# Decoder layer: twenty sets of weight sums instead of ten, formed in DRAM by accumulating DMAs

## Chip, cores and metric

The kernel runs on one core of one Trainium2 chip. The metric is the device time of one execution in microseconds; lower is better.

## The reference

One decoder layer in float32 on 256 tokens of width 2048: a SwiGLU feed-forward (inner width 5632), a mixer (sliding-window attention beside an RWKV-7 recurrence), cross-attention into a memory of 256 tokens, and a second feed-forward.

```python
def swiglu(h, w_gate, w_up, w_down):
    return (jax.nn.silu(h @ w_gate) * (h @ w_up)) @ w_down
...
x = x + 0.5 * swiglu(rms_norm(x, ffn1_norm[l]), ffn1_w_gate[l], ffn1_w_up[l], ffn1_w_down[l])
x = gated_parallel_mixer(x, ...)
x = memory_cross_attention(x, mem, ...)
x = x + 0.5 * swiglu(rms_norm(x, ffn2_norm[l]), ffn2_w_gate[l], ffn2_w_up[l], ffn2_w_down[l])
return rms_norm(x, final_norm)
```

## The kernel before

**Three-pass products.** Every product of activations and weights is made of three matmuls. Both factors are split into a high part (`hi`, rounded to the matmul's float32r format by ScalarE, L400) and a rest (`lo`, L401, VectorE), and `times` (L477 to L479) multiplies hi by hi, lo by hi and hi by lo into one accumulator bank. A matmul is 128 x 128 by 128 x 512.

**Items.** The weights come from DRAM in units of two row chunks (128 rows each) by 512 columns, split as they come. In the feed-forwards the gate and the up matrix (or two column blocks of the down matrix) are worked together. There an *item* is a pair of such units, `g` and `u`, and multiplies two row chunks with two token halves: four block products of two chunks, 8 x 3 = 24 matmuls. A block of 512 columns has eight items, q = 0 to 7. `next_item` prepares one item ahead of TensorE.

**Seven products.** For some q (`SEVEN` in the first feed-forward, `SEVEN_2` in the second) the 2 x 2 block product is made with seven products instead of eight, in the manner of Strassen and Winograd: 21 matmuls. That needs four sums of the weight chunks (`divide`, L429 to L432, VectorE), which are split in turn (`two_parts`, L408 and L409, tiles `thi` and `tlo`, one buffer each), and sums of the activations, made once (`combinations`, L509 to L528, tile parts `chi` and `clo`). The products go to the banks p1 to p7; `middle` (L614 to L616) and `out` (L623 to L628) put them together. `x` holds the first feed-forward's or the second's token block, and `rs` is the reciprocal root of the norm, made on GpSimd (L714) and read by Silu (L753 in the first column block, L624 in the others).

**Staged sums.** In the second feed-forward, q = 3 of each of ten column blocks (`STAGED`) doesn't form its sums in place. They were formed during the mixer: `stage` loads the gate's and the up matrix's chunks into two tiles (L380), makes four subtractions on VectorE (L384 to L389) and stores the four sums to the DRAM tensor `sums` (L392). `load_sums` (L369) loads them two items ahead into two `raw` buffers of a ring of four, which the sums formed in place and the activations' sums use too.

**Order.** All weights are loaded by SP's queue, in one order, into four `raw2` buffers of 1 MB in the feed-forwards. Side work is written as generators that `Interleave` steps between the items of the main work (`bg.spawn`, `bg.tick`); `stage` is one of them and begins at item `STAGE_AT`. The stepping sets where an instruction is recorded. The framework then places the instructions on each engine's queue by its own order, with waits for data and buffers; it holds an instruction back only where `issue_after` names one to wait behind. GpSimd's queue has, in the first feed-forward, the constants, `rs`, the fetches of the small vectors (L254, L293) and the stores of x (L828).

Of the kernel before, what the change touches and what calls it, by code (L numbers as in the profile page):

```python
# [8 lines left out]
F32R = mybir.dt.float32r  # L9
# [127 lines left out]
def decoder_layer(ctx: ExitStack, tc: tile.TileContext, a: dict, out: bass.AP):  # L137
# [175 lines left out]
    for entry in weight_plan(a):  # L313
        if entry is None:
            ends.append(len(units))
            continue
        plan.append(entry)
        w, k0, nk, c0, n = entry
        if not isinstance(w, tuple):
            for k in range(k0, k0 + nk, KU):  # L320
                items.append(((len(units),), False))
                units.append((w, k, c0, n))
            continue
        for k in range(k0, k0 + nk, 2 * KU):
            u = len(units)
            units += [(v, k + i, c, 512) for v, c in zip(w, c0) for i in (0, KU)]
            for i in range(2):
                q = (k - k0) // KU + i
                if n == SEVEN_2 and q in STAGED:
# [3 lines left out]
    first_unused = {items[i][0][1] for i in staged}  # L333
    sums_d = dram.tile([len(staged), P, 4, 512], F32, name="sums")
    at = {"item": 0, "product": 0, "pool": None}

    def load(u, pieces=None):

        if u >= len(units) or u in raws:
            return  # L340
        w, k, c0, n = units[u]
        wide = at["pool"] is not None and (u < ends[0] or u >= ends[1] + LOADED)
        m = 2 if wide else 1
        if wide:
            raw = at["pool"].tile([P, m * KU, n], F32, tag="raw2", name="raw2", bufs=4)
# [4 lines left out]
        if u in first_unused:  # L350
            second = u + 1 in first_unused
            pieces = [(slice(1, 2), nc.sync)] + [(slice(2 + second, 4), nc.sync)]
            if not second:
                pieces = ((slice(1, 4), nc.sync),)
        elif u + 1 in first_unused and wide:
            pieces = ((slice(0, 2), nc.sync), (slice(3, 4), nc.sync))
        for i, queue in pieces or ((slice(0, m * KU), nc.sync),):
            rows = slice((k + i.start) * P, (k + i.stop) * P)
            queue.dma_start(raw[:, i], w[rows, c0 : c0 + n].rearrange("(a p) n -> p a n", p=P))

    def load_sums(i):

        if i not in staged or i in summed:
            return
        summed[i] = [
            wp.tile([P, KU, 512], F32, tag="raw", name="raw", bufs=4) for _ in range(2)
        ]
        for e, t in enumerate(summed[i]):
            nc.sync.dma_start(t[:], sums_d[staged[i], :, KU * e : KU * e + KU, :])  # L369

    def stage(t4, i, n):


        while at["item"] < STAGE_AT[n]:
            yield
        t = t4("su", (P, KU, 512)), t4("sg", (P, KU, 512))
        for e, v in zip(t, items[i][0][::-1]):
            w, k, c0, _ = units[v]
            rows = slice(k * P, (k + KU) * P)
            nc.sync.dma_start(e[:], w[rows, c0 : c0 + 512].rearrange("(a p) n -> p a n", p=P))  # L380
        yield from idle(4)
        u0, u1, g0, g1 = (e[:, c] for e in t for c in range(KU))
# [3 lines left out]
        yield  # L386
        with tc.issue_after(at["lo"].ins):
            dve.tensor_tensor(u1, u1, g0, ALU.subtract)
            dve.tensor_tensor(g1, g1, u1, ALU.subtract)  # L389
        yield from idle(8)  # L390
        for c, e in enumerate(t):
            nc.sync.dma_start(sums_d[n, :, KU * c : KU * c + KU, :], e[:])  # L392

    def split_unit(u, rows=slice(0, KU)):
        n, raw = units[u][3], raws[u]
# [5 lines left out]
            at["lo"] = dve.tensor_tensor(lo[:, s], raw[:, s], f32(hi[:, s]), ALU.subtract)  # L401
        return hi, lo

    def two_parts(v, e):
        sp = at["pool"]
        hi = sp.tile([P, KU, 512], F32R, tag="thi" + e, name="thi")
        lo = sp.tile([P, KU, 512], F32R, tag="tlo" + e, name="tlo")
        act.copy(hi[:], v[:])  # L408
        dve.tensor_tensor(lo[:], v[:], f32(hi[:]), ALU.subtract)  # L409
        return hi, lo  # L410

    def divide(i):


        if i >= len(items) or i in parts:
            return
        which, seven = items[i]
        if len(which) == 1:
            parts[i] = split_unit(*which)
            return  # L420
        g, u = which
        if not seven:
            parts[i] = split_unit(g), split_unit(u)
            return
        t = summed.get(i)
        if t is None:
            rg, ru = raws[g], raws[u]
            t = [wp.tile([P, KU, 512], F32, tag="raw", name="raw", bufs=4) for _ in range(2)]
            dve.tensor_tensor(t[1][:, 0], ru[:, 0], rg[:, 0], ALU.subtract)  # L429
            dve.tensor_tensor(t[0][:, 0], ru[:, 1], ru[:, 0], ALU.subtract)  # L430
# [58 lines left out]
    def combinations(sp, x: Act, seven, name, ready=lambda: True, early=True, n=0):  # L489
# [8 lines left out]
        def work():  # L498
# [3 lines left out]
            for q in pairs:  # L502
# [9 lines left out]
                    )  # L512
                if q in seven:
                    n = 4
                    dve.tensor_tensor(f[:, 0], v[:, 0, 1], v[:, 1, 1], ALU.add)
                    dve.tensor_tensor(f[:, 1], f[:, 0], v[:, 0, 0], ALU.subtract)
                    dve.tensor_tensor(f[:, 2], v[:, 0, 0], v[:, 0, 1], ALU.subtract)
# [19 lines left out]
    def product_pair(x: Act, c, w, first, middle, out):  # L537
# [28 lines left out]
        for q in range(nk // KU):  # L566
            k = KU * q
            if q in seven:
# [2 lines left out]
                end = q == max(seven)  # L571
                ta, tb = s
                for i, (to, x_, w_) in enumerate((
                    ("p7", of_c(q, 2), of_w(ta, 0)), ("p6", of_c(q, 1), of_w(ta, 1)),
                    ("p1", of_x(0, k), of_w(g, 0)), ("p2", of_x(0, k + 1), of_w(g, 1)),
                    ("p3", of_c(q, 3), of_w(u, 1)), ("p4", of_x(1, k + 1), of_w(tb, 1)),
                    ("p5", of_c(q, 0), of_w(tb, 0)),
                )):
                    add(to, x_, w_, end and to in ("p1", "p5", "p6", "p7"))
                    if i % 2:  # L580
                        bg.tick()
                    if end and to == "p1":
                        first(b)
# [21 lines left out]
    def gate_and_up(sp, x: Act, c, r, w):  # L605
# [5 lines left out]
            act.copy(hb[:, 0], b["p1"][:])  # L611

        def middle(b):
            dve.tensor_tensor(u2[:], b["p6"][:], hb[:, 0], ALU.add)  # L614
# [5 lines left out]
        def out(b, to):  # L620
            t = int(to in ("p4", "p5"))
            if to in ("p2", "p4"):
                dve.tensor_tensor(hb[:, t], b[to][:], u3[:] if t else hb[:, 0], ALU.add)  # L623
# [9 lines left out]
    def down(sp, h: Act, c, w, xs):  # L633

        u2, u3 = sums_of(sp)

        def half(x_, v):
            dve.scalar_tensor_tensor(x_, v, 0.5, x_, ALU.mult, ALU.add)

        def first(b):  # L640
            act.copy(u3[:], b["p1"][:])
# [1 line left out]
            half(xs[1][1], b["q"][:])  # L643

        def middle(b):
            dve.tensor_tensor(u2[:], b["p6"][:], u3[:], ALU.add)
            dve.tensor_tensor(u3[:], b["p7"][:], u2[:], ALU.add)
            dve.tensor_tensor(u2[:], b["p5"][:], u2[:], ALU.add)
            half(xs[1][0], u3[:])
            half(xs[1][1], u3[:])  # L650
            half(xs[0][1], u2[:])

# [65 lines left out]
    def feed_forward(sp, x, norm: Norm, wg, wu, wd, done, begin_last=lambda: None, last=False):  # L718
        if last:
            for tag, shape, dt, bufs in (  # L720
                ("hhi", [P, 16, T], F32R, 1), ("hlo", [P, 16, T], F32R, 1),
                ("hb", [P, 2, 512], F32, 2), ("thia", [P, KU, 512], F32R, 1),
                ("tloa", [P, KU, 512], F32R, 1), ("thib", [P, KU, 512], F32R, 1),
                ("tlob", [P, KU, 512], F32R, 1),
            ):
                sp.tile(shape, dt, tag=tag, name=tag, bufs=bufs)
        begun = at["item"]
# [76 lines left out]
    with tc.tile_pool(name="f1", bufs=1, reuse_waits="tile") as sp:  # L804
# [32 lines left out]
    with tc.tile_pool(name="mx", bufs=1, reuse_waits="tile") as sp:  # L837
# [6 lines left out]
        for i, n in staged.items():  # L844
            bg.spawn("stage", stage(t4, i, n))

        def act_tiles(name, n):
            return Act(
# [845 lines left out]
```

## Time and profile before

| | |
|---|---|
| time, median of 3 runs | 2246.25 us (2245.61 to 2247.01) |
| span of the profiled execution, first to last instruction | 2242.8 us |
| median less that span | 3.45 us |
| TensorE busy | 2228.0 us, 10587 matmuls |
| VectorE busy | 1824.9 us |
| ScalarE busy | 1248.6 us |
| GpSimd busy | 129.8 us |
| moved by DMA | 461.84 MB, mean 206 GB/s |
| granted TensorE clock | 0.999 |

The page gives the profiled execution's time as its span alone; what lies around it is in the difference to the median. A busy share of TensorE counts overlapping matmuls, so the rate is read from their starts in the timeline. A row of the windows gives, for each engine, the busy time in that stretch with the number of instructions, then the granted clock, the busy share of the DMA engines and GB/s.

### The profile page before, as it was taken

What the parts mean: (1) busy time and instruction counts of PE and PEld (TensorE: products, weight loads), DVE (VectorE), ACT (ScalarE), POOL (GpSimd) and SP (SyncE); (2) the same over time, 40 slices, a digit from 0 to 9 for tenths busy, and PEclk for the clock granted to TensorE, in tenths of its full rate; (3) what the DMA queues carried; (4) which work ended last, traced back from release to release, by engine and by line L of the source; (5) the groups of instructions that cost most, each with busy time, mean ns of one, the idle gap of its engine ahead of it and who ended that gap; (6) DMA issues with size and microseconds to landing.
All of it is one profiled execution on the core that took longest, in us unless ns stands there. A gap on an engine that the chain in (4) does not pass through costs nothing.

```text
span 2242.8 us, 28283 instructions
## 1 busy us (share of the span) xinstructions
PE 2228.0 (99%) x10587; PEld 1830.8 (82%) x10587; DVE 1824.9 (81%) x2365; ACT 1248.6 (56%) x1629; POOL 129.8 (6%) x197
## 2 busy tenths in 40 slices
PE   9999999999999999999999999999999999999998
PEld 7888888888888877788888888888888888888886
DVE  7898988998989476977657656547999999999997
ACT  6555555555556468544434546456565466555654
POOL 1000000000001001200321030001000000000000
PEclk9999999999999999999999999999999999999999
DMA  7555555555555544676668576547565566556564
GB/s 264 188 199 197 204 195 201 203 189 206 193 201 197 170 137 152 193 233 212 207 214 281 194 260 231 188 167 272 199 234 205 199 231 220 201 200 227 197 226 150
DMA packets 229705, 461.84 MB, mean 206 GB/s; under 512 B 15467, under 2 KB 17744, under 8 KB 229568
## 3 DMA queue, kind: packets, MB, share of 16 engines
q1 hardware_dynamic: 220512, 433.62, 56.7%
q0 software_dynamic: 8592, 25.62, 3.7%
q8 instruction: 83, 1.36, 0.2%
q10 hardware_dynamic: 464, 0.79, 0.1%
q14 instruction: 54, 0.44, 0.1%
HBM read 436.30 MB, written 23.59 MB: 205 GB/s over the span
## 4 chain that ended last, share of the span: by engine, by line
PE 97%; DVE 1%; DMA 1%; issue 1%; ACT 0%; SPq 0%; POOL 0%; POOLq 0%; DVEq 0%
PE acc L477 20%; PE acc L478 19%; PE acc L479 19%; PE mm L478 8%; PE mm L479 8%; PE mm L477 8%; PE tr L665 2%; PE tr L478 2%; PE tr L477 2%; PE tr L479 2%; PE mm L1349 1%; PE tr L1285 1%; DVE lo L401 0%; PE mm L912 0%; DMA raw<-in_ffn_w_gate_dram 0%
## 5 line engine op out<-in xcount | busy, mean ns | idle before, releaser
L400 ACT CAST hi<-raw 128x1024 fp32r<-128x1024 f32 (+1 forms) x770 | 756.2, 992 | 710.3 <-PE acc L479 509.5
L401 DVE TENSOR_TENSOR lo<-raw,hi 128x1024 fp32r<-128x1024 f32 (+1 forms) x770 | 882.4, 1149 | 307.7 <-ACT hi L400 306.0
L477 PE MATMUL acc<-hi,xhi 128*128 128x512 f32 (+1 forms) x1166 | 461.4, 396 | 2.5 <-ACT xhi L692 2.1
L478 PE MATMUL acc<-lo,xhi 128*128 128x512 f32 (+1 forms) x1166 | 452.9, 388 | 0.0
L479 PE MATMUL acc<-hi,xlo 128*128 128x512 f32 (+1 forms) x1166 | 452.4, 388 | 0.0
L477 PEld LDWEIGHTS acc<-hi,xhi 128*128 128x128 f32 x1166 | 219.3, 188 | 50.6 <-issue 4.0
L479 PEld LDWEIGHTS acc<-hi,xlo 128*128 128x128 f32 x1166 | 218.8, 188 | 45.7 <-DVE xlo L693 1.0
L478 PEld LDWEIGHTS acc<-lo,xhi 128*128 128x128 f32 x1166 | 219.2, 188 | 43.8 <-issue 1.7
L408 ACT CAST thi<-raw 128x1024 fp32r<-128x1024 f32 x192 | 199.7, 1051 | 62.2 <-DVE raw L431 41.8
L409 DVE TENSOR_TENSOR tlo<-raw,thi 128x1024 fp32r<-128x1024 f32 x192 | 232.3, 1219 | 1.2 <-ACT thi L408 0.4
L479 PE MATMUL acc<-hi,hlo 128*128 128x512 f32 x372 | 145.5, 391 | 0.0
L478 PE MATMUL acc<-lo,hhi 128*128 128x512 f32 x372 | 145.4, 391 | 0.0
L477 PE MATMUL mm<-hi,xhi 128*128 128x512 f32 x370 | 145.4, 393 | 0.0
L477 PE MATMUL acc<-hi,hhi 128*128 128x512 f32 x372 | 144.9, 390 | 0.0
L479 PE MATMUL mm<-hi,xlo 128*128 128x512 f32 x370 | 144.3, 390 | 0.0
L478 PE MATMUL mm<-lo,xhi 128*128 128x512 f32 x370 | 144.2, 390 | 0.0
L478 PEld LDWEIGHTS acc<-lo,hhi 128*128 128x128 f32 x372 | 69.9, 188 | 14.3
L477 PEld LDWEIGHTS acc<-hi,hhi 128*128 128x128 f32 x372 | 69.9, 188 | 14.3
L479 PEld LDWEIGHTS acc<-hi,hlo 128*128 128x128 f32 x372 | 69.9, 188 | 14.0
L479 PEld LDWEIGHTS mm<-hi,xlo 128*128 128x128 f32 x370 | 69.4, 188 | 14.5
L478 PEld LDWEIGHTS mm<-lo,xhi 128*128 128x128 f32 x370 | 69.5, 188 | 14.2
L477 PEld LDWEIGHTS mm<-hi,xhi 128*128 128x128 f32 x370 | 69.5, 188 | 14.1
(410 smaller groups left out, 3601.1 us busy)
## 6 DMA issues: line engine op xcount, KB each, us to landing
raw<-in_ffn_w_down_dram SPq DMA_DIRECT2D x88, 1024.0 KB, 5.2
raw<-in_ffn_w_gate_dram SPq DMA_DIRECT2D x84, 1024.0 KB, 5.1
raw<-in_ffn_w_up_dram SPq DMA_DIRECT2D x78, 1024.0 KB, 6.4
raw<-in_w_in_dram SPq DMA_DIRECT2D x136, 512.0 KB, 3.5
raw<-in_w_out_dram SPq DMA_DIRECT2D x32, 512.0 KB, 4.4
raw<-sums SPq DMA_DIRECT2D x20, 512.0 KB, 6.2
raw<-in_w_proj_attn_dram SPq DMA_DIRECT2D x16, 512.0 KB, 3.9
raw<-in_w_proj_rwkv_dram SPq DMA_DIRECT2D x16, 512.0 KB, 5.6
```

Of the source, the lines that this page charges most:

```text
L400: at["hi"] = act.copy(hi[:, s], raw[:, s])
L401: at["lo"] = dve.tensor_tensor(lo[:, s], raw[:, s], f32(hi[:, s]), ALU.subtract)
L408: act.copy(hi[:], v[:])
L409: dve.tensor_tensor(lo[:], v[:], f32(hi[:]), ALU.subtract)
L477: pe.matmul(o, xh, hi, start=first, stop=False, **how)
L478: pe.matmul(o, xh, lo, start=False, stop=False, **how)
L479: pe.matmul(o, xl, hi, start=False, stop=last, **how)
L665: pe.transpose(b[:, o : o + P], tok[:, t, col : col + P], ident[:])
L1285: pe.matmul(b[e][:, o : o + P], x1[r, j, cs_], x2[r, j, cs_], start=True, stop=True)
L1349: pe.matmul(vb[:, (o + k) * P : (o + k + 1) * P][:, r], lhs(k, e), rhs[:, k, r], start=first and k + e == 0, stop=True, **ek,)
```

## The change

The second feed-forward has seven products in five of eight items (q = 0, 2, 3, 4, 5) instead of four, in each of ten column blocks. The sums of two of them, q = 3 and q = 5, are staged: twenty sets.

The sums are not formed during the mixer any more, on VectorE, but from the first feed-forward on, by DMAs from DRAM to DRAM on GpSimd's queue, some of them accumulating into their target. A set takes eight DMAs of 256 KB in six steps: t1 <- u0 and t3 <- u0; t1 += g0 and t3 += u1; t2 <- t1; t2 += u1; t4 <- t2; t4 += g1. The generators begin at items 18, 23, and so on to 113 of the first feed-forward.

An accumulating DMA only adds, so the signs of the weights' sums change everywhere, and those of the activations' sums and of the put-together with them. t1 takes the place of the chunk u0 that the seven products don't use (in place, L429, or loaded there from `sums`), so `u` is now split whole and the second tile of sums has one chunk instead of two.

```diff
-SEVEN_2, STAGED = (0, 2, 3, 4), (3,)
+SEVEN_2, STAGED = (0, 2, 3, 4, 5), (3, 5)
-STAGE_AT = [266 + 2 * n for n in range(10)]
+STAGE_AT = [18 + 5 * n for n in range(20)]
...
+        for v in first:
+            nc.sync.dma_start(raws[v][:, 0], sums_d[first_sums[v], :, 0, :])
...
-        for e, t in enumerate(summed[i]):
-            nc.sync.dma_start(t[:], sums_d[staged[i], :, KU * e : KU * e + KU, :])
+        for t, c, m in zip(summed[i], (1, 3), (2, 1)):
+            nc.sync.dma_start(t[:, :m], sums_d[staged[i], :, c : c + m, :])
-    def stage(t4, i, n):
+    def stage(i, n):
         while at["item"] < STAGE_AT[n]:
             yield
-        t = t4("su", (P, KU, 512)), t4("sg", (P, KU, 512))
-        for e, v in zip(t, items[i][0][::-1]):
-            ...
-            nc.sync.dma_start(e[:], w[rows, c0 : c0 + 512].rearrange("(a p) n -> p a n", p=P))
...
-        with tc.issue_after(at["lo"].ins):
-            dve.tensor_tensor(g0, u0, g0, ALU.subtract)
-            dve.tensor_tensor(u0, u1, u0, ALU.subtract)
...
-        for c, e in enumerate(t):
-            nc.sync.dma_start(sums_d[n, :, KU * c : KU * c + KU, :], e[:])
+        t1, t2, t3, t4 = (sums_d[n, :, c, :] for c in range(4))
...
+        for steps in (
+            ((t1, u0), (t3, u0)), ((t1, g0), (t3, u1)), ((t2, t1),), ((t2, u1),), ((t4, t2),),
+            ((t4, g1),),
+        ):
+            for to, of in steps:
+                if of is u0 or of is t1 or of is t2:
+                    pool.dma_start(to, of)
+                else:
+                    pool.dma_start(to, of, accum_op=ALU.add)
+            yield from idle(8)
...
-            dve.tensor_tensor(t[1][:, 0], ru[:, 0], rg[:, 0], ALU.subtract)
-            dve.tensor_tensor(t[0][:, 0], ru[:, 1], ru[:, 0], ALU.subtract)
-            dve.tensor_tensor(t[0][:, 1], ru[:, 1], t[1][:, 0], ALU.subtract)
-            dve.tensor_tensor(t[1][:, 1], rg[:, 1], t[0][:, 1], ALU.subtract)
-        a_ = two_parts(t[0], "a")
-        parts[i] = split_unit(g), split_unit(u, slice(1, 2)), (a_, two_parts(t[1], "b"))
+            dve.tensor_tensor(ru[:, 0], ru[:, 0], rg[:, 0], ALU.add)
+            dve.tensor_tensor(t[0][:, 0], ru[:, 1], ru[:, 0], ALU.add)
+            dve.tensor_tensor(t[0][:, 1], t[0][:, 0], rg[:, 0], ALU.subtract)
+            dve.tensor_tensor(t[1][:, 0], t[0][:, 0], rg[:, 1], ALU.add)
+        a_ = two_parts(t[0], "a", 2)
+        parts[i] = split_unit(g), split_unit(u), (a_, two_parts(t[1], "b", 1))
...
                 for i, (to, x_, w_) in enumerate((
-                    ("p7", of_c(q, 2), of_w(ta, 0)), ("p6", of_c(q, 1), of_w(ta, 1)),
+                    ("p7", of_c(q, 2), of_w(ta, 1)), ("p6", of_c(q, 1), of_w(ta, 0)),
...
-                    ("p3", of_c(q, 3), of_w(u, 1)), ("p4", of_x(1, k + 1), of_w(tb, 1)),
-                    ("p5", of_c(q, 0), of_w(tb, 0)),
+                    ("p3", of_c(q, 3), of_w(u, 1)), ("p4", of_x(1, k + 1), of_w(tb, 0)),
+                    ("p5", of_c(q, 0), of_w(u, 0)),
...
         bg.spawn("const", late_vectors())
+        for i, n in staged.items():
+            bg.spawn("stage", stage(i, n))
```

More of the change, by code (lines that the diff above doesn't have):

```diff
@@ L328, in decoder_layer @@
                 q = (k - k0) // KU + i
-                if n == SEVEN_2 and q in STAGED:
+                if len(ends) == 2 and n == SEVEN_2 and q in STAGED:
                     staged[len(items)] = len(staged)
@@ L349, in load @@
             raws[u + i] = raw[:, i * KU : (i + 1) * KU, :]
[L350 to L356, printed above, removed]
+        first = [v for v in (u, u + 1)[:m] if v in first_sums]
+        for v in first:
+            nc.sync.dma_start(raws[v][:, 0], sums_d[first_sums[v], :, 0, :])
+        if first:
+            pieces = ((slice(1, 4), nc.sync),)
+            if first[0] > u:
+                pieces = ((slice(0, 2), nc.sync), (slice(3, 4), nc.sync))
+            elif len(first) == 2:
+                pieces = ((slice(1, 2), nc.sync), (slice(3, 4), nc.sync))
         for i, queue in pieces or ((slice(0, m * KU), nc.sync),):
@@ L402, in split_unit, with two_parts @@
         return hi, lo
-    def two_parts(v, e):
+    def two_parts(v, e, n):
         sp = at["pool"]
[L406 to L409, printed above, removed]
+        hi = sp.tile([P, n, 512], F32R, tag="thi" + e, name="thi")
+        lo = sp.tile([P, n, 512], F32R, tag="tlo" + e, name="tlo")
+        act.copy(hi[:], v[:, :n])
+        dve.tensor_tensor(lo[:], v[:, :n], f32(hi[:]), ALU.subtract)
         return hi, lo
@@ L622, in out @@
             if to in ("p2", "p4"):
-                dve.tensor_tensor(hb[:, t], b[to][:], u3[:] if t else hb[:, 0], ALU.add)
+                if t:
+                    dve.tensor_tensor(hb[:, 1], b[to][:], u3[:], ALU.subtract)
+                else:
+                    dve.tensor_tensor(hb[:, 0], b[to][:], hb[:, 0], ALU.add)
                 act.activation(hb[:, t], hb[:, t], AF.Silu, scale=r[t])
@@ L635, in down, with half @@
         u2, u3 = sums_of(sp)
-        def half(x_, v):
-            dve.scalar_tensor_tensor(x_, v, 0.5, x_, ALU.mult, ALU.add)
+        def half(x_, v, by=0.5):
+            dve.scalar_tensor_tensor(x_, v, by, x_, ALU.mult, ALU.add)
         def first(b):
@@ L645, in middle @@
         def middle(b):
[L646 removed]
+            dve.tensor_tensor(u2[:], b["p6"][:], u3[:], ALU.subtract)
             dve.tensor_tensor(u3[:], b["p7"][:], u2[:], ALU.add)
             dve.tensor_tensor(u2[:], b["p5"][:], u2[:], ALU.add)
[L649 removed]
+            half(xs[1][0], u3[:], -0.5)
             half(xs[1][1], u3[:])
```

29 lines of the change are left out of this document (11 added, 18 removed).

## The prediction

> **What bounds the kernel now.** I read the page, then five-microsecond to fifty-microsecond windows, then the timelines of each engine.
>
> ```profile
> span 2242.8 us, 28283 instructions
> PE 2228.0 (99%) x10587; PEld 1830.8 (82%) x10587; DVE 1824.9 (81%) x2365; ACT 1248.6 (56%) x1629; POOL 129.8 (6%) x197
> PE 97%; DVE 1%; DMA 1%; issue 1%; ACT 0%; SPq 0%; POOL 0%; POOLq 0%; DVEq 0%
> ```
>
> TensorE is busy 99% of the span and owns 97% of the chain that ended last. Busy time alone would not prove that it runs at its peak, so I take the start-to-start time from the timeline. The profiled execution spans 2242.8 us; the runs' median is 2246.25, 3.45 us more. I sum against the span and add 3.45.
>
> ```profile
> 1816.60 0.39 PE L477 MATMUL acc<-hi,xhi 128*128 128x512 f32 x1
> ...
> 1832.72 0.39 PE L479 MATMUL mm<-hi,xlo 128*128 128x512 f32 x1
> ```
>
> These are the first and the last of 72 matmuls in a row, so 71 steps take 16.12 us: 0.227 us each. That is the price of a matmul while nothing starves TensorE. The windows show how near the vector engine is to being the next bound:
>
> ```profile
> 1819.00:1861.00 42.00, 42.00 (x188) 34.36 (x187) 38.56 (x46) 25.35 (x28) 0.00 (x0) 1.00 0.60 213
> 1903.00:1945.00 42.00, 42.00 (x189) 34.26 (x188) 41.24 (x54) 26.16 (x30) 0.00 (x0) 1.00 0.59 212
> ```
>
> Columns: PE, PEld, DVE, ACT, POOL busy, clock, DMA share, GB/s. In the second feed-forward DVE is busy 92 to 98%.
>
> **The gain: matmuls.** A pair of chunks costs 24 matmuls (four products, two chunks, three passes); with seven products 21. Ten column blocks of the second feed-forward get one more such pair: 10 x 3 = 30 matmuls less (the built programs differ by exactly 30 of this shape), 30 x 0.227 = **-6.8 us** if nothing else is late.
>
> **The gain: the mixer's staging.** It goes altogether: 20 loads and 20 stores of 512 KB from SP's queue, 40 DVE subtractions.
>
> ```profile
> 1106.43 7.74 DMA sg<-in_ffn_w_gate_dram
> 1110.00:1114.00 4.00, 3.68 (x25) 2.92 (x24) 3.23 (x4) 0.59 (x1) 0.00 (x0) 1.00 1.05 329
> 1114.00:1118.00 4.00, 3.23 (x24) 2.59 (x22) 3.71 (x6) 1.57 (x3) 0.00 (x0) 1.00 1.00 370
> 1177.00:1191.00 14.00, 14.00 (x102) 10.99 (x101) 12.05 (x16) 8.54 (x12) 5.72 (x10) 1.00 1.03 307
> ```
>
> The first row is the chain's wait for the first staging load. TensorE then idles 0.32 + 0.77 = 1.09 us; later staging shows no idle. So **-1.1 us**, between 0 (something else is late there next) and the 7.7 of the wait.
>
> **What the vector engine takes back.** The new pair is split as seven half-chunk rows (g 2, u 2, the two sums 2 and 1), not four.
>
> ```profile
> 1754.91 0.69 DVE L429 TENSOR_TENSOR raw<-raw,raw 128x512 f32<-128x512 f32 x1
> 1755.52 0.69 DVE L430 TENSOR_TENSOR raw<-raw 128x512 f32<-128x512 f32 x1
> ...
> 1828.16 2.35 DVE L409 TENSOR_TENSOR tlo<-raw,thi 128x1024 fp32r<-128x1024 f32 x2
> 1830.43 1.22 DVE L401 TENSOR_TENSOR lo<-raw,hi 128x1024 fp32r<-128x1024 f32 x1
> ...
> 1834.56 1.41 DVE L628 SCALAR_TENSOR_TENSOR hb<-u,rs,hb 128x512 f32<-128x512 f32 x2
> 1835.88 1.22 DVE L401 TENSOR_TENSOR lo<-raw,hi 128x1024 fp32r<-128x1024 f32 x1
> 721.52 0.87 PE tr L665 x8
> PEld tr L478 <- DVE tlo L409: 4.2, 13, 0.4
> raw<-sums SPq DMA_DIRECT2D x20, 512.0 KB, 6.2
> ```
>
> Back to back, a 512-wide DVE operation takes 0.61 us, a 1024-wide one 2.27/2 = 1.135, a scalar_tensor_tensor 0.66. A block now has 20 wide, 25 narrow (4 splits of u, 12 sums, 3 + 2 + 2 at the end of a block, 2 for transposes) and 2 of the last: 22.7 + 15.2 + 1.3 = 39.2 us, against TensorE's 180 x 0.227 + 0.87 (eight transposes) = 41.7. The other seven-pairs move one row from the second sum to u: nothing. The new pair makes two wide splits into three wide and one narrow: +1.75 us. After: DVE 41.0, TensorE 177 x 0.227 + 0.87 = 41.0. A dead heat: any idle of DVE now shows. Already before, matmuls of sums waited 4.2 us for L409 in 13 places. The new set is also loaded through the same ring of four `raw` buffers, behind two 1 MB loads, and lands 6.2 us after issue, so it comes about when its split is due. Bounds of the loss: 0 (DVE keeps its lead) to 15 us (1.5 us in each of ten blocks). I take **+2.5 us**, nearest to the 4.2 of the waits row. ScalarE (26 of 42 us) has room. The second feed-forward reads 30 x 256 KB = 7.9 MB more, at a DMA share of 0.60: nothing. The sixth pair of x's combinations, some 3 us of DVE, lies in the first column block of the second feed-forward, which has no seven-pairs and so DVE idle; without that cover it costs 3.
>
> **What is added: 160 copies on GpSimd's queue.** Each set is eight copies of 256 KB from DRAM to DRAM, five of them accumulating. `STAGE_AT` orders the building of the program; it puts no wait into it. A copy waits only for copies before it, and GpSimd is idle, so in the program as built the copies stand at the front of GpSimd's queue. The first one stands ahead of `ident`, and **34 stand ahead of `rs`**, the norm's reciprocal root. Who waits for that:
>
> ```profile
> 0.98 0.10 POOL L305 MEMSET nhalf<- 128x2 f32 x1
> 32.85 0.70 POOL L714 TENSOR_TENSOR rs<-ms,nhalf 128x2 f32<-128x2 f32 x1 [31.45 <-DVE ms L712]
> 33.51 0.74 POOL L293 DMA_DIRECT2D sinks<-in_attn_sinks_dram  x1
> 33.74 1.28 ACT L753 ACT_TABLE_LOAD   x1
> 35.04 1.26 ACT L753 ACTIVATE hb<-acc,rs 128x512 f32<-128x512 f32 x2
> ```
>
> The first Silu (L753) reads `rs`. It empties the accumulator bank that the second half of the next product's first chunk wants (three `acc` banks, two held), and all of ScalarE's later casts queue behind it. The first half is 6 matmuls, 1.36 us, from about 35.1 (Silu's own start, when the second bank of the first product ends), so TensorE stops at 36.5 unless Silu's first half is done. `rs` takes 0.70 and that half some 0.7: TensorE's stall is (start of `rs`) - 35.
>
> The queue stops at nearly every copy for the one four places before it (a step of the same set). 34 copies are thus about 8 landings, plus some 4 us (start at 1, four issues of 0.74). No row shows a DRAM-to-DRAM or an accumulating copy; the nearest are GpSimd's other DMAs:
>
> ```profile
> L828 POOL DMA_DIRECT2D x1d<-x x4: 707/724/777, 684.0 to 718.4; - x4
> DMA to landing us min/median/max: 3.3/5.7/13.2
> ...
> L1510 POOL DMA_DIRECT2D mem<-in_mem_dram x4: 722/723/724, 1343.6 to 1345.7; - x4
> DMA to landing us min/median/max: 7.8/9.8/11.8
> ...
> L1262 POOL DMA_DIRECT2D xb<-xd x16: 582/582/612, 1097.0 to 1180.3; - x16
> DMA to landing us min/median/max: 2.0/4.8/8.2
> ...
> wa<-in_rwkv_w_dram POOLq DMA_DIRECT2D x1, 256.0 KB, 4.3
> 5.00:25.00 20.00, 17.90 (x87) 13.53 (x86) 12.72 (x20) 15.02 (x31) 0.00 (x0) 1.00 1.04 387
> ```
>
> While the DMA engines are full even the 32 KB `xb` copies take up to 8.2; otherwise 256 KB take 4.3. From 5 to 25 us they are full (share 1.04), and the copies prolong that. I take one landing of 4.5, three of 8.1, four of 4.5: 46.8, so `rs` starts at 46.8 + 4 = 51 and the stall is **+16 us**. Bounds: 8 x 3.3 + 4 = 30, no stall; 8 x 11.8 + 4 = 98, 63 us of it. The Trainium skill, "DMA: Bandwidth & Descriptors", section "Issuing engines are not separate DMA queues", says that DMAs of all queues share sixteen engines and interleave; the longer `xb` landings at a share of 1.03 agree.
>
> The rest of the queue at the start: `ident` comes one issue (0.74) later and is wanted only once the gain vector has landed; the fetches of the other gain vectors (from 33.51) move back with `rs`, and so does the matmul work ahead of their transposes: nothing. The first loads of x and weights share the full engines and land later too, within the same stall.
>
> The Trainium skill, "TensorE: Matmul & The Clock Gate", part 1, says that an idle window of some 3.4 us halves the clock for as long again; by it the stall would cost an estimated 1.7 us more, and no window of before can show it.
>
> After `rs` 126 copies follow. The four `mem` transfers landed over (11.8 - 7.8) + 3 x 0.72 = 6.2 us, so 256 KB in 1.03 us; 126 take at least 130 us, in which the weights' loads share full engines. From 1177 to 1191 the share was 1.03 and TensorE lost nothing; from 1110 to 1118 it lost 14%, which over 130 us would be 18. I take **+3**, range 0 to 18, nearer the first, since part of the second was staging's own wait. GpSimd is free long before 684, its next work.
>
> Sum: -6.8 - 1.1 + 2.5 + 16 + 3 = +13.6; span 2256.4, time **2259.9 us**.
>
> **Rivals.** (1) *Short landings.* If copies land in 3.8 us or less, `rs` is issued by 35 and nothing at the start is late: -6.8 - 1.1 + 2.5 = -5.4, 2240.8 us; 2238.3 if DVE loses nothing. For it: `x1d` at 3.3. Against: the full engines from 5 to 25. Beside it, the Trainium skill, "DMA: Bandwidth & Descriptors", section "Anatomy of one DMA — SWDGE (gpsimd) path", gives 2.0 us plus bytes at 436 GB/s, an estimated 2.6 us for 256 KB, and by that no stall; the longer rows above speak against it here. Chance 0.28.
> (2) *The second feed-forward becomes DVE's.* Without a stall at the start, the loss there eats the gain: from 0.7 us in each block on, 2246 and up to 2253. For it: the dead heat. Against: DVE's lead carries over an item. Chance 0.09.
> (3) *Accumulating copies are twice as slow*, because they read both sides: landings of 9 to 12, `rs` at 76 to 100, and 250 us of full engines: +41 to +65 and twice the 3: 2284 to 2314. Nothing in the trace speaks for it but the bound of 11.8. Chance 0.13.
>
> **The numbers.** My forecast has 0.50. It reaches from 2244 (landings of 4.5) to 2280. The range 2240 to 2288 leaves out most of rival 3 and the best of rival 1, under 0.2 in all. No change means within 0.2%, 4.5 us, about what can be told apart. Faster by more: most of rival 1, 0.22. Same: its rest, half of rival 2 and the forecast's low end, 0.13. Slower: 0.65.
>
> **What would show it.** Right: `rs` on POOL starts far later than 32.85, Silu waits for POOL, TensorE has one gap of over 10 us before 60 us, and the first feed-forward is otherwise whole. DVE near 41 of 42 us in the second feed-forward, 30 matmuls fewer, the mixer 1 us shorter. Wrong: `rs` before 36 us; or TensorE's losses spread over 50 to 250 us (then loads, not `rs`); or idle of ten like sizes in the second feed-forward.

## The result: 5.8% slower, and where the 129 us are

The changed kernel takes 2375.4 us (median of 4 runs, 2370.32 to 2382.51) against 2246.05 us before (median of 4 runs): a ratio of 1.0577, 95% interval 1.0564 to 1.0591. The forecast was 2259.9 with a range to 2288. The direction came out as forecast, the size did not. The profiled execution took 2370.32 us, with a span of 2368.5.

The page of the changed kernel first, with the lines that answer to those of the prediction: span, TensorE's row, the chain by engine, the two large DMA queues (packets, MB, share of 16 engines' span) and two groups of VectorE with their waits.

```profile
span 2368.5 us, 28518 instructions
PE 2261.0 (95%) x10557; PEld 1841.1 (78%) x10557; DVE 1825.7 (77%) x2351; ACT 1261.3 (53%) x1650; POOL 239.7 (10%) x357
q1 hardware_dynamic: 216832, 420.52, 54.1%
q0 software_dynamic: 26512, 67.57, 12.3%
PE 75%; DMA 12%; DVE 9%; issue 2%; ACT 1%; SPq 0%; POOL 0%; POOLq 0%; DVEq 0%; ACTq 0%
L401 DVE TENSOR_TENSOR lo<-raw,hi 128x1024 fp32r<-128x1024 f32 (+1 forms) x770 | 932.2, 1215 | 351.2 <-ACT hi L400 348.7
L429 DVE TENSOR_TENSOR raw<-raw,raw 128x512 f32<-128x512 f32 x86 | 58.8, 684 | 77.2 <-DMA raw<-in_ffn_w_up_dram 61.1
```

The same two queues in the kernel before:

```profile
q1 hardware_dynamic: 220512, 433.62, 56.7%
q0 software_dynamic: 8592, 25.62, 3.7%
```

TensorE owns 75% of the chain instead of 97%, and DMA owns 12% instead of 1%. L429, the first of the sums of weights, waits 61.1 us for the up matrix to land; what it makes goes on through the split to the matmuls.

To see which stage lost, I take two instructions that begin a stage: ScalarE's first read of a mixer product (`tok`) and the first Silu of the second feed-forward. In these rows of the timeline by form, before and after, the stage begins at the first number behind the durations.

```profile
L856 ACT ACTIVATE tok<-acc,rs x22: 515/690/694, 737.7 to 1479.8; 128x512 f32<-128x512 f32 x20, 128x288 f32<-128x288 f32 x2
L753 ACT ACTIVATE hb<-acc,rs x2: 682/686/689, 1559.3 to 1559.9; 128x512 f32<-128x512 f32 x2
```

```profile
L858 ACT ACTIVATE tok<-acc,rs x22: 515/690/696, 857.5 to 1599.2; 128x512 f32<-128x512 f32 x20, 128x288 f32<-128x288 f32 x2
L756 ACT ACTIVATE hb<-acc,rs x2: 682/686/689, 1678.8 to 1679.4; 128x512 f32<-128x512 f32 x2
```

The table has these stages for all kernels; below, only rows on which a verdict rests are shown again.

| kernel | first feed-forward | mixer | second feed-forward | ratio to before, 95% interval |
|---|---|---|---|---|
| before | 737.7 | 821.6 | 683.5 | 1 |
| changed | 857.5 | 821.3 | 689.7 | 1.0564 to 1.0591 |
| rs first | 849.4 | 820.8 | 691.7 | 1.0504 to 1.0547 |
| plain copies | 810.6 | 821.1 | 690.9 | 1.0333 to 1.0374 |
| ten sets | 813.2 | 820.5 | 687.1 | 1.0328 to 1.0365 |
| paced | 776.6 | 820.2 | 689.9 | 1.0205 to 1.0249 |
| paced, long | 754.3 | 832.6 | 692.2 | 1.0121 to 1.0155 |
| sums by VectorE | 739.0 | 849.8 | 692.0 | 1.0141 to 1.0172 |
| the same, gapped pairs | 739.0 | 849.6 | 686.5 | 1.0130 to 1.0160 |
| the same, sums on GpSimd's queue | 738.9 | 848.4 | 684.2 | 1.0113 to 1.0143 |
| the same, less VectorE work | 739.2 | 847.9 | 693.0 | 1.0152 to 1.0186 |
| spread, gapped, GpSimd's queue | 738.8 | 832.5 | 694.7 | 1.0077 to 1.0105 |
| before, sums on GpSimd's queue | 737.6 | 820.8 | 688.3 | 1.0010 to 1.0027 |

Each row of stages is one execution, the profiled one, and the runs of one kernel differ by up to 12 us (changed and paced), 7 (paced, long) or some 4 (the kernels with sums by VectorE). A difference of a few us between two rows counts only where the medians of the runs show it too.

So 119.8 us go in the first feed-forward, none in the mixer, 6.2 in the second feed-forward. Windows of the changed kernel show how the first of these is spread (columns as in the prediction):

```profile
0.00:50.00 50.00, 37.25 (x147) 28.38 (x148) 20.79 (x36) 24.41 (x48) 15.49 (x30) 0.90 1.01 283
50.00:100.00 50.00, 28.02 (x114) 22.36 (x113) 23.61 (x38) 14.94 (x21) 22.57 (x36) 0.76 0.90 222
150.00:200.00 50.00, 34.34 (x120) 27.13 (x121) 30.78 (x37) 18.02 (x20) 16.66 (x25) 0.76 1.00 239
300.00:350.00 50.00, 41.39 (x165) 33.02 (x166) 41.77 (x55) 21.18 (x23) 12.61 (x18) 0.90 1.01 265
350.00:400.00 50.00, 50.00 (x221) 41.13 (x220) 46.53 (x55) 26.48 (x28) 1.35 (x2) 1.00 0.69 221
```

For as long as the copies run, the DMA engines are full (shares of 0.90 to 1.03) and TensorE makes 114 to 185 matmuls in 50 us instead of some 225. Losses spread over 50 to 250 us are what the prediction named as a sign that loads, not `rs`, are the cause. When the copies are done (the last is issued at 356.5), all is as before. These are the accumulating half of the copies, by form, and the landings of all 160:

```profile
L391 POOL DMA_DIRECT2D sums<-in_ffn_w_gate_dram x40: 800/837/1187, 9.3 to 356.5; - x40
L391 POOL DMA_DIRECT2D sums<-in_ffn_w_up_dram x40: 805/828/1222, 10.9 to 341.2; - x40
DMA to landing us min/median/max: 3.8/8.3/13.2
```

### The profile page after: what moved, and what is told of

Same layout as the page of the kernel before. It is cut to its first block, busy times and chain, and to the rows that moved or that the text cites. A ratio compares the mean times of both kernels' runs of the same rounds, so it can differ in the third digit from the quotient of the medians.

```text
span 2368.5 us, 28518 instructions
## 1 busy us (share of the span) xinstructions
PE 2261.0 (95%) x10557; PEld 1841.1 (78%) x10557; DVE 1825.7 (77%) x2351; ACT 1261.3 (53%) x1650; POOL 239.7 (10%) x357
## 3 DMA queue, kind: packets, MB, share of 16 engines
q0 software_dynamic: 26512, 67.57, 12.3%
HBM read 475.62 MB, written 55.05 MB: 224 GB/s over the span
## 4 chain that ended last, share of the span: by engine, by line
PE 75%; DMA 12%; DVE 9%; issue 2%; ACT 1%; SPq 0%; POOL 0%; POOLq 0%; DVEq 0%; ACTq 0%
PE acc L477 16%; PE acc L478 16%; PE acc L479 16%; PE mm L479 5%; PE mm L478 5%; DMA raw<-in_ffn_w_up_dram 5%; PE mm L477 5%; DVE lo L401 4%; DMA raw<-sums 2%; PE tr L668 2%; PE tr L478 2%; PE tr L477 2%; PE tr L479 1%; DMA raw<-in_ffn_w_down_dram 1%; DMA sums<-in_ffn_w_up_dram 1%
## 5 line engine op out<-in xcount | busy, mean ns | idle before, releaser
L400 ACT CAST hi<-raw 128x1024 fp32r<-128x1024 f32 (+1 forms) x770 | 804.5, 1046 | 780.6 <-PE acc L479 490.8
L401 DVE TENSOR_TENSOR lo<-raw,hi 128x1024 fp32r<-128x1024 f32 (+1 forms) x770 | 932.2, 1215 | 351.2 <-ACT hi L400 348.7
L477 PEld LDWEIGHTS acc<-hi,xhi 128*128 128x128 f32 x1136 | 216.7, 191 | 79.6 <-ACT hb L756 22.4
L408 ACT CAST thi<-raw 128x1024 fp32r<-128x1024 f32 x212 | 169.3, 833 | 91.1 <-DVE raw L431 71.4
L409 DVE TENSOR_TENSOR tlo<-raw,thi 128x1024 fp32r<-128x1024 f32 x212 | 196.3, 950 | 4.8 <-ACT thi L408 4.1
L477 PE MATMUL mm<-hi,xhi 128*128 128x512 f32 x340 | 135.4, 398 | 1.4 <-ACT hi L400 1.4
L479 PE MATMUL mm<-hi,xlo 128*128 128x512 f32 x340 | 134.1, 394 | 0.0
L429 DVE TENSOR_TENSOR raw<-raw,raw 128x512 f32<-128x512 f32 x86 | 58.8, 684 | 77.2 <-DMA raw<-in_ffn_w_up_dram 61.1
L478 PE MATMUL mm<-lo,chi 128*128 128x512 f32 x220 | 87.2, 396 | 12.5 <-DVE lo L401 12.5
L479 PE MATMUL mm<-hi,clo 128*128 128x512 f32 x220 | 86.7, 394 | 0.0
L477 PE MATMUL mm<-hi,chi 128*128 128x512 f32 x220 | 86.1, 394 | 0.0
```

The source lines that it names most:

```text
L400: at["hi"] = act.copy(hi[:, s], raw[:, s])
L408: act.copy(hi[:], v[:, :n])
L409: dve.tensor_tensor(lo[:], v[:, :n], f32(hi[:]), ALU.subtract)
L429: dve.tensor_tensor(ru[:, 0], ru[:, 0], rg[:, 0], ALU.add)
L477: pe.matmul(o, xh, hi, start=first, stop=False, **how)
L478: pe.matmul(o, xh, lo, start=False, stop=False, **how)
```

## Experiments

**Theory.** The 160 copies overfill the DMA engines. The rival that I had forecast as the main loss is `rs` behind 34 copies. In the second feed-forward the question is whether its 6.2 us are VectorE's load, late sums, or something that the copies leave behind.

### rs first

```diff
+with tc.issue_after(at["fetched"].ins):     # last fetch of the vectors, itself behind rs
     pool.dma_start(to, of ...)
```

> Every copy for the sums now stands behind the first normaliser (rs) and the vectors' fetches on GpSimd's queue; the number of copies and their spacing stay. Theory A (the 160 copies, bunched, fill the DMA engines, about 1.46 us of all 16 for each, and the weight loads of the first feed-forward starve): only the early stall goes, rs returns from 71.8 us to about 33-40, the flood starts later by about 35 us and lasts as long; the first feed-forward ends at 815-835 us instead of 857.5 (before: 737.7), total 2325-2350. Rival B (the place of rs in the queue is the main loss, as the prediction had it): the first feed-forward ends at 740-775, total 2250-2290.

Measured: 2362.92 us. Two rows of `rs` and of the mixer's start:

```profile
L721 POOL TENSOR_TENSOR rs<-ms,nhalf x1: 702/702/702, 32.8 to 32.8; 128x2 f32<-128x2 f32 x1
L862 ACT ACTIVATE tok<-acc,rs x22: 513/690/695, 849.4 to 1590.7; 128x512 f32<-128x512 f32 x20, 128x288 f32<-128x288 f32 x2
```

`rs` is back at 32.8, where it was before the change, 39 us earlier, and the stage ends only 8.1 us earlier (the medians are 12.5 us apart). That is a smaller gain even than the theory's (815 to 835). A delay that is taken away at the start is paid again: the copies that had run during that stall now run beside the weights.

This kernel gives a clean account of the full engines, since the copies begin after 42 us. One window of 350 us, of the kernel before and of this one:

```profile
50.00:400.00 350.00, 350.00 (x1567) 289.15 (x1566) 318.81 (x391) 195.37 (x219) 0.00 (x0) 1.00 0.57 195
```

```profile
50.00:400.00 350.00, 268.67 (x1069) 211.62 (x1068) 219.35 (x269) 131.24 (x148) 105.36 (x154) 0.88 0.99 251
```

1069 of 1567 matmuls are 239 us of progress, so 111 us are lost (the stage lost 111.7). That progress needs 0.57 x 239 = 136 us of the DMA engines for weights. They were busy 0.99 x 350 = 346, so 210 went to copies. The queue rows of the page say the same from the other side: q0 grew from 0.037 x 2242.8 = 83 to 0.123 x 2368.5 = 291 us, by 208, or 1.30 us of all 16 engines for a copy. (The expectation's 1.46 comes out if every copy is counted as 128 packets of 182 ns; the shares give 1.30.) 136 + 208 = 344: in this window the loss is DMA time that did not fit. The packets of this window in the trace, added up by queue, say the same: 138 us for q1 and 207 for q0.

### Plain copies

```diff
-pool.dma_start(to, of, accum_op=ALU.add)
+pool.dma_start(to, of)
```

> All 160 copies are plain ones; the additions are left out, so the sums are wrong, but the same bytes go between the same places at the same points of the program, with the same order in the queue. If it is the accumulation that makes the added packets dear (about 182 ns of an engine for 2 KB against about 92 for a weight load): the packets of that queue fall to 90-110 ns, the copies end at 200-260 us instead of 356, the first feed-forward ends at 785-815, total 2300-2330. Rival: moving from DRAM to DRAM is what is dear, with or without the addition: packets stay at 160-185 ns, copies end at 320-356, the first feed-forward ends at 840-858, total 2350-2372.

```profile
q0 software_dynamic: 21392, 67.57, 9.7%
L858 ACT ACTIVATE tok<-acc,rs x22: 515/690/692, 810.6 to 1552.1; 128x512 f32<-128x512 f32 x20, 128x288 f32<-128x288 f32 x2
```

Measured: 2324.32 us. The megabytes are the same, but q0's time falls to 0.097 x 2322.6 = 225 us, so 142 for the copies: 0.89 us each. Of the 160, 80 accumulate (four in each set of eight; the prediction's "five" was a miscount). They then take (208 - 80 x 0.89) / 80 = 1.71 us each: an accumulating copy holds the engines 1.9 times as long as a plain one. The packets in the trace of the changed kernel show it directly: a plain copy goes in 64 packets of 4 KB, of 0.220 us each on one engine, an accumulating one in 128 packets of 2 KB, of 0.211 us each. That is 0.88 and 1.69 us of all 16 engines. So the expectation had the right range for the time, but not for the packets, which it saw at 90 to 110 ns: without the addition there are fewer of them (80 for a copy instead of 112, those of 4 bytes included), and an average one still takes 0.178 us, 0.186 in the changed kernel. A weight load takes 0.567 x 2242.8 / 433.62 MB, or 0.77 us for 256 KB, so a plain copy is not much dearer than a load. The stage's loss falls from 119.8 to 72.9, as forecast. The copies ended later than forecast (last issued at 294.2, not 200 to 260): GpSimd still sat idle for 189 us in all, waiting for earlier copies to land.

### Ten sets

```diff
-SEVEN_2, STAGED = (0, 2, 3, 4, 5), (3, 5)
+SEVEN_2, STAGED = (0, 2, 3, 4), (3,)
```

> The changed kernel with the four pairs of before (0, 2, 3, 4; sums from DRAM for 3 alone): ten sets and 80 copies instead of 20 and 160, formed in the same way at the same pace from the same start. Theory (the loss of the first feed-forward is the copies' time on full DMA engines): about half of it stays, the copies end at 175-205 us, the first feed-forward ends at 785-805 (before 737.7, after 857.5). Rival (the loss comes from the start alone, the late rs and what follows): it ends above 830. The second feed-forward, without its fifth pair, is back at 682-685 us, total 2290-2315.

```profile
L756 ACT ACTIVATE hb<-acc,rs x2: 682/686/690, 1633.7 to 1634.3; 128x512 f32<-128x512 f32 x2
```

Measured: 2322.71 us. Half of the copies, ended as forecast (last issue at 186.4), but 63% of the loss (75.5 of 119.8 us): above the forecast for the stage and for the total (2290 to 2315). Its first windows show why:

```profile
0.00:50.00 50.00, 36.83 (x146) 28.00 (x147) 20.49 (x35) 24.11 (x48) 15.55 (x30) 0.90 1.00 277
50.00:100.00 50.00, 26.85 (x112) 21.48 (x111) 23.65 (x39) 15.18 (x20) 22.76 (x36) 0.76 0.91 230
```

Up to 100 us it makes 258 matmuls, the changed kernel 261 and the kernel before 441, so some 41 us of loss are common to both; only what comes later (35 us here, some 79 in the changed kernel) goes with the number of copies. In the first 50 us the DMA share is 0.80 even before the change, so there the copies find the least room. The second feed-forward takes 687.1 us with the four pairs of before, not 683.5. So the new form of the sums alone (other signs, `u` split whole, the sums' loads ahead of the weights on SP's queue) costs 3.6 us there, where the expectation had none (682 to 685).

### Paced copies

```diff
+with tc.issue_after(at["hi"].ins):          # behind the weights' split now due
+    act.copy(mark[:, k], ones[:, :1])
+with tc.issue_after(at["fetched"].ins):
+    seen = pool.tensor_copy(marked[:, k], mark[:, k])
+with tc.issue_after(seen.ins):
     pool.dma_start(to, of ...)
-STAGE_AT = [18 + 5 * n for n in range(20)]
+STAGE_AT = [10 + 6 * n for n in range(20)]
```

> The same copies, behind rs, but each step of a set waits (through a tiny copy on ScalarE and one on GpSimd) for the weights' split then due, and the sets begin six weight items apart, so that the copies are spread over some 680 us of the first feed-forward (demand on the DMA engines about 0.58 + 0.34 = 0.92 of the time). Theory A (bunching overfills the engines): the first feed-forward ends at 740-765 us, the DMA share stays under 1 in most windows, total 2250-2280. Rival C (a copy costs TensorE time however thinly it is spread, since each delays the weight load that it meets): the first feed-forward still ends above 790, total above 2300. In both the second feed-forward stays at 689-690 us.

In the second kernel the sets are 13 items apart (`18 + 13 * n`), the late ones begun in the mixer:

> As in the paced kernel, with the sets 13 weight items apart, over the first feed-forward and the mixer (some 1,350 us, demand about 0.60 + 0.17). Theory A: the first feed-forward ends within 737-745 us, the mixer takes 821-828, and what is left is the second feed-forward's own change: 689-690 us there (before 683.5), total 2246-2258. Rival C: both stages together still lose over 60 us, total above 2310. Rival D (the second feed-forward's 6 us are an after-effect of the flood and not of its own work): it takes 676-684 us there and the total is 2236-2247.

Measured: 2297.43 and 2276.95 us. Windows of the paced kernel, then the mixer's worst one of the long-paced kernel:

```profile
50.00:720.00 670.00, 646.15 (x2824) 518.08 (x2823) 575.92 (x707) 358.86 (x508) 182.95 (x277) 1.00 0.89 249
```

```profile
900.00:1000.00 100.00, 93.14 (x431) 73.71 (x431) 70.98 (x76) 48.12 (x67) 41.54 (x48) 0.97 0.89 244
```

Spreading the same 160 copies takes the loss of the first feed-forward from 119.8 to 38.9 us, so bunching was most of it; the forecast (at most 27) was too good. (The profiled execution of the paced kernel is the fastest of its four; by the medians the whole loss falls from 129.4 to 52.6 us.) At a share of 0.89 the engines are not full on average, yet loads that meet a copy land late: the first sums of the weights wait 55.9 us for the up matrix in this stage, 8.2 before.

```profile
DVE raw L439 <- DMA raw<-in_ffn_w_up_dram: 55.9, 20, 5.7
```

The small copies that set the pace cost little: ScalarE waits 1.1 us in all for GpSimd to read them. Nor does a copy get cheaper by being spread: by the queue's row (13.9% of 2286.7 us) it takes 1.47 us of the engines here. Still thinner (long pace), 16.6 us remain there and 11.0 come back in the mixer. So neither expectation holds whole: the loss falls with the spacing, but at mean shares of 0.73 to 0.89 a copy that meets a load goes on costing something. Rival D falls: with the copies spread out the second feed-forward is no better (689.9 and 692.2).

### Sums by VectorE

The sums are formed in the mixer as before the change, now 20 sets with the new signs; no accumulating copies.

```diff
-t1, t2, t3, t4 = (sums_d[n, :, c, :] for c in range(4))    # and the eight copies
+t = t4("su", ...), t4("sg", ...)                           # two loads, four adds, three stores
-STAGE_AT = [18 + 5 * n for n in range(20)]
+STAGE_AT = [206 + 5 * n for n in range(20)]
```

> No accumulating copy: the 20 sets are formed by VectorE during the mixer, as the kernel before formed its ten, with the signs of the change; the five pairs of the second feed-forward stay. Theory (the formation cost the 120 us, the fifth pair has a cost of its own in the second feed-forward): the first feed-forward is back at 737-739 us, the mixer takes 822-830, the second feed-forward 688-693 (before 683.5; the paced kernels 689.9 and 692.2), total 2246-2258. Rival (the second feed-forward's loss comes from the accumulating copies, by what they leave behind): it takes 675-680, total 2234-2243.

Measured: 2280.09 us. The first feed-forward is back at 739.0: without the copies its loss is gone, and the new signs cost it 1.3 us at most. The mixer's 849.8 us were not expected (822 to 830): the new sets stand in stretches that have little room (a share of 0.95 in the window below), and other places for them, in the last experiment, bring 832.5.

```profile
1000.00:1100.00 100.00, 95.37 (x422) 76.92 (x421) 89.37 (x115) 40.39 (x43) 8.77 (x10) 1.00 0.95 331
```

The second feed-forward's loss is its own (692.0, as forecast), and three edits of this kernel ask why. Gapped pairs:

```diff
-SEVEN_2, STAGED = (0, 2, 3, 4, 5), (3, 5)
+SEVEN_2, STAGED = (0, 1, 2, 4, 5), (1, 4)
```

> As the kernel with sums by VectorE, but the seven-product pairs of the second feed-forward are 0, 1, 2, 4, 5, with sums from DRAM for 1 and 4: no more than three of them in a row (before the change three, 2 to 4; in the change four, 2 to 5), and the costly ones (sums formed on the spot) at 0, 2 and 5. Theory V (VectorE can't keep up over four such items in a row): the second feed-forward falls to 676-684 us, total 2236-2248. Rival Q (the sums from DRAM land late, wherever they stand): it stays at 687-693.

The loads of the last three sums of each set on GpSimd's queue (the first one's stays among the weights' loads):

```diff
-nc.sync.dma_start(t[:, :m], sums_d[staged[i], :, c : c + m, :])
+pool.dma_start(t[:, :m], sums_d[staged[i], :, c : c + m, :])
```

> As the kernel with sums by VectorE, but the loads of the last three sums of each set are issued by GpSimd, which is idle in the second feed-forward, instead of by SyncE behind the weights' loads. Rival Q (the sums from DRAM land late because of their place on SyncE's queue): ScalarE's wait for them (10 to 12 us in 7 or 8 times in the changed and the paced kernels) goes below 3 us, the second feed-forward falls to 677-685. Theory V (VectorE): it stays within 1.5 us of the kernel with sums by VectorE.

Less VectorE work (`lo = hi` for the fourth sum):

> As the kernel with sums by VectorE, with the low part of the fourth sum left out in the second feed-forward (its high part is multiplied in its place, so the matmuls stay the same and the output is wrong there): 100 VectorE instructions of 0.68 us fewer, 68 us of its some 640. Theory V (VectorE): the second feed-forward falls by 5 us or more, to 676-685. Rival Q (late sums): it falls by less than 2 us.

Measured: 2277.99, 2273.57 and 2281.96 us. Waits in the second feed-forward (total, times, longest), first with the sums loaded by SP, then by GpSimd:

```profile
PEld tr L480 <- ACT thi L411: 14.3, 29, 1.3
PEld tr L481 <- DVE tlo L412: 6.5, 16, 1.0
ACT thi L411 <- DMA raw<-sums: 11.5, 9, 2.9
```

```profile
PEld tr L481 <- DVE tlo L412: 6.0, 19, 0.6
PEld tr L480 <- ACT thi L411: 5.5, 21, 0.4
ACT thi L411 <- PE tr L482: 12.5, 18, 1.6
```

ScalarE's split of the sums waits 11.5 us for them to land, and TensorE 14.3 us for that split. On the other queue the wait for the DMA is no longer among the largest, and the stage takes 684.2 us, 7.8 less (6.5 by the medians, and the runs of the two kernels do not overlap). Taking work off VectorE does not shorten the stage, although it was 541.97 us busy in 600 instead of 575.25 (the kernel with sums by VectorE, then with less of its work):

```profile
1600.00:2200.00 600.00, 592.79 (x2605) 477.13 (x2604) 575.25 (x704) 358.36 (x406) 2.17 (x4) 1.00 0.66 225
```

```profile
1600.00:2200.00 600.00, 590.39 (x2599) 476.62 (x2599) 541.97 (x641) 360.39 (x404) 2.17 (x4) 1.00 0.66 225
```

So late sums are shown as the larger part of that loss in this kernel; VectorE's load is not shown, and not excluded either. The edit took off 33 us in that window, about half of what the expectation counted on, and the waits for loads grew at the same time (late sums from 11.5 to 16.2 us, weights for the sums formed in place from 1.6 to 9.4). The gap brought 5.5 us in the profiled executions, with the wait for late sums still at 12.3, but only 2.1 by the medians, with intervals that overlap: too little to decide anything.

### All together, and the old kernel with the new queue

> The sums by VectorE again, ten sets from the mixer's first items on (stretches where the profile before shows the DMA engines at 0.50) and ten near those of before; the gapped pairs (0, 1, 2, 4, 5) and GpSimd's queue for the sums' loads together. Theory (the mixer's 28 us in the kernel with sums by VectorE were 20 sets met by weight loads in stretches at 0.84 and 0.95; the second feed-forward's loss is late sums and the run of four, and the two add up): mixer 822-833, second feed-forward 677-682, total 2240-2254. Rival (the sets cost the mixer their time wherever they stand): mixer above 840, total above 2258.

> The kernel before with one edit: the loads of its ten sets' sums in the second feed-forward are issued by GpSimd instead of SyncE. The kernel before shows no wait for late sums among its larger ones and some 5 us of stalls of TensorE in that stage, so at most a little is to be had: second feed-forward 680-684 (before 683.5), total 2242-2247, a ratio of 0.9985 to 1.0005.

The first has `STAGE_AT = [143 + 5 * n if n < 10 else 246 + 2 * n for n in range(20)]`, the gapped pairs and GpSimd's queue; the second is the kernel before with GpSimd's queue alone. Measured: 2265.86 and 2249.02 us, both above what was expected (2240 to 2254, 2242 to 2247). Rows of the first one:

```profile
740.00:800.00 60.00, 60.00 (x314) 50.52 (x312) 37.92 (x53) 30.06 (x48) 0.00 (x0) 1.00 0.94 310
DVE raw L432 <- DMA raw<-in_ffn_w_up_dram: 12.2, 6, 3.2
ACT thi L411 <- DVE raw L434: 18.3, 15, 3.9
```

The mixer came out as forecast at 832.5 (822 to 833), still 10.9 us above before, but the two edits of the second feed-forward do not add up: 694.7 us against a forecast of 677 to 682, and no better than without either (692.0). Now the sums come in time and the weights for the sums that are formed on the spot don't (L432 waits 12.2 us, 1.6 in the kernel with the sums on SP). In the kernel before, GpSimd's queue costs 4.8 us (4.1 by the medians), and there too L429's wait for weights grew from 5.4 to 11.0 us. That an early load of sums takes the engines from the next weights' load would explain both; it was not tested by itself. No version with five pairs came below before: its best second feed-forward, 684.2, is not shorter than the 683.5 of four pairs, so there was nothing to pay for the sums with.

## Why the prediction failed, point by point

- **The 126 copies after `rs`: +3, range to 18. This is the step that failed.** With `rs` back in its place the copies alone cost the first feed-forward 111.7 us. Their own price was not far off: 1.03 us taken from the `mem` transfers, 1.30 measured. What was wrong was to read the loss from rows of 14 us (none) and 8 us (14%) of full engines and to hold it for 130 us, instead of adding up what copies and weights need of the same engines; that loads issued ahead cover so short a stretch is the likely reason for the small loss there, but no run isolates it. The copies then took 285 us, not 130. At the prediction's own price 160 copies need 160 x 1.03 = 165 us of the engines. The window of 350 us with `rs` first had 239 us of progress, in which the weights leave 0.43 x 239 = 103 us free, so some 60 do not fit; with the measured 208 it is 105, and 111 were lost. Nothing paces copies that wait only for each other.
- **`rs` at 51, stall +16.** The mechanism was right, the sizes off: 34 copies do stand ahead of `rs`, but it starts at 71.8, and Silu waits 22.4 us for it. Eight landings of the measured median, 8.3 us, and the 4 us of issues make 70; the prediction took five of the eight at 4.5.

```profile
71.80 1.03 POOL L717 TENSOR_TENSOR rs<-ms,nhalf 128x2 f32<-128x2 f32 x1
72.86 1.27 ACT L756 ACTIVATE hb<-acc,rs 128x512 f32<-128x512 f32 x2 [22.41 <-POOL rs L717]
```

  But the stall is not a term to be added: taking it away gave back 8 us (12.5 by the medians). The prediction counted the stall and the contention as two prices, and they are one DMA budget.
- **Rival 3** (accumulation twice as slow, since it reads both sides) was right in the price: 1.71 us against 0.89. Its reason is not shown: the pages of the changed kernel and of the plain copies give the same bytes read from DRAM, 475.62 MB, and what the trace shows is packets half as large that take as long. It was given 0.13, and its sum is 2288 to 2312 by its own terms, not 2284 to 2314; even that was too low, since it kept the same small price for full engines. (Four copies of a set accumulate, not the prediction's five.)
- **The matmuls, -6.8:** 30 fewer (10557), so the saving itself is there. TensorE's stalls took it back: adding up what each start-to-start step of the second feed-forward has over 0.227 us gives 5.0 us before and 16.8 after. -6.8 + 11.8 = 5.0 of the 6.2 measured.
- **VectorE in the second feed-forward, +2.5, bounds to 15:** the value within its bounds was too low (some 12 to 13 us were lost), and the cause that it priced, a dead heat of VectorE, was not shown. The waits name late sums (the changed kernel's second feed-forward, then TensorE's wait there before), and 3.6 us come with the new form already with four pairs. The text had the late sums ("comes about when its split is due") but priced the other. That the sums' place in the queue is the cause was tried in the kernel with sums by VectorE, not in the changed kernel itself.

```profile
PEld tr L477 <- ACT thi L408: 11.3, 29, 1.6
ACT thi L408 <- DMA raw<-sums: 10.3, 7, 2.8
```

```profile
PEld tr L477 <- ACT thi L408: 1.4, 5, 0.4
```

- **The mixer's staging, -1.1:** 821.6 to 821.3 us, so at most a third of that.
- **Clock:** priced at an estimated 1.7 us for one stall; there were eleven start-to-start steps over 3.4 us in the changed kernel's first 357 us, and see below.

## What to carry over

Copies that wait only for each other run as fast as the DMA engines let them: ask what they need in engine time (share of the queue times the span), what the main work leaves free over the same stretch, and what is over is the loss. "In the background" needs a real dependence on the work's progress, and even then a kernel fed just in time loses something where a copy meets a load that it waits for. And before paying for an input to save matmuls, look whether the matmuls' place has room to take it on time.

## What was not expected of the hardware

An accumulating copy from DRAM to DRAM held the 16 engines 1.71 us for 256 KB, a plain one 0.89, a load to SBUF 0.77; the accumulating one goes in 2 KB packets, the plain one in 4 KB packets, and each packet takes some 0.21 to 0.22 us. The Trainium skill, "DMA: Bandwidth & Descriptors", section "Issuing engines are not separate DMA queues", says that DMAs of all issuers run on the same sixteen engines and interleave; the account above (136 us of SP's loads and 208 of GpSimd's copies in 346 busy) agrees.

Each long stall also slowed what came after it. After 6.21 us of idle in the changed kernel:

```profile
121.23 0.79 PE L478 MATMUL acc<-lo,xhi 128*128 128x512 f32 x1 [6.21 <-DVE lo L401]
...
122.25 0.63 PE L477 MATMUL acc<-hi,xhi 128*128 128x512 f32 x1
122.67 0.63 PE L478 MATMUL acc<-lo,xhi 128*128 128x512 f32 x1
...
126.45 0.39 PE L478 MATMUL mm<-lo,chi 128*128 128x512 f32 x1
```

For 5 us the steps are 0.427 us instead of 0.227, and the granted clock in the windows falls to 0.76. Up to 357 us there are 101 such steps: 101 x 0.2 = 20 us of TensorE's loss of some 120, about 2 us for each stall. The Trainium skill, "TensorE: Matmul & The Clock Gate", part 1, gives an idle window of about 3.4 us as what drops the clock and some 3.4 us as the time until it is back; the stalls here bear out the first in the main (every idle of 3.6 us or more was followed by slow steps, and so were some shorter ones, of 2 to 3 us), and the second was some 3 to 6.5 us in these traces.
